# Stick-breaking attention weights as running products, two heads' logits from 64 rows each, and finishes issued in later parts

## The chip, the cores and the metric

The kernel runs on one core of a Trainium2 chip. The metric is the device time of one execution in microseconds (us). Engines are named as the profile names them: PE is TensorE (matmuls; PEld its weight loads), DVE is VectorE, ACT is ScalarE, POOL is GpSimd, SP is SyncE, whose queue issues most DMA transfers. A matmul of float32 operands shows in the trace as two passes, one of the rounded format fp32r as one.

## What is computed

One transformer layer on 512 tokens of width 1024 (16 meta tokens stand ahead of them): a projection, two mixers side by side (HGRN2 with 4 heads, stick-breaking attention with 8 heads of 64), the output projection with residual and layer norm, and a mixture of 16 experts with a second layer norm. The change touches the stick-breaking mixer and the two norms behind it.

```python
def head_rms_norm(x, g):
    xf = x.astype(jnp.float32)
    y = xf * lax.rsqrt(jnp.mean(xf * xf, axis=-1, keepdims=True) + RMS_EPS)
    return y.reshape(*x.shape[:-2], -1) * g

def stick_breaking_mixer(q, k, v, norm_g):
    ...
    for blk in range(Lp // Q_BLOCK):
        ...
        z = jnp.einsum('bhqd,bhkd->bhqk', qh[:, :, start:end], kh[:, :, :end])
        mask = jnp.arange(end)[None, :] < (start + jnp.arange(Q_BLOCK))[:, None]
        log_keep = jnp.where(mask, jax.nn.log_sigmoid(-z), 0.0)
        log_a = jax.nn.log_sigmoid(z) + lax.cumsum(log_keep, axis=3, reverse=True) - log_keep
        a = jnp.where(mask, jnp.exp(log_a), 0.0)
        outs.append(jnp.einsum('bhqk,bhkd->bhqd', a, vh[:, :, :end]))
    o = jnp.concatenate(outs, axis=2).transpose(0, 2, 1, 3)
    return head_rms_norm(o, norm_g)
```

So the weight of a key is sigmoid(z) of that key, times the product of sigmoid(-z) over all later keys that the query may see.

## The kernel before, in words

The kernel runs in stages: the input projection (7 groups of 512 columns), into whose last groups the HGRN2 heads are woven; then **the stick-breaking stage**, into which the output projection is woven (`weave`, ratio WO_RATIO); then the rest of the output projection with the router (which expert each token goes to); then the 16 experts, whose weights stream from HBM, and the second norm.

The stick-breaking stage has three units of query tiles (UNITS): tile 3 with 528 keys, tile 2 with 400, and tiles 0 and 1 together (144 and 272 keys, 416 columns). Within a unit the 8 heads go in pairs `pr` of two heads `s`; `sb_weights` makes one head's weights, `sb_values` transposes them (PE into bank `tr`, then a copy to the tile `aT`) and multiplies them with the values, and `sb_finish` normalises a group of heads and splits it in a high and a low half for the output projection. In the tiles, `z` of the code is a PSUM bank of the four named `pj`; `t` is the tag of `ll` (2 buffers), `zs` that of `cc` (3 buffers), `am` holds the weights of the meta keys.

The logits of one head are matmuls whose weights (`sqZ`) have 128 rows, of which 64 hold the head's query and 64 are zero, since the two heads of a pair share the 128 rows of `skT`. Each head then takes, on ACT, Abs, Exp, Ln and a last Exp, on DVE a Relu (a quarter of them on ACT), the reversed running sum (`tensor_tensor_scan`) and a subtraction from the logits, so that a `pj` bank is held until that subtraction. `rsqrt` is Ln and Exp on ACT with one Newton step on DVE in the norm of a token, and Ln and Exp alone in `sb_finish`.

`out_proj` multiplies the mixers' outputs with the output weights: `wo_half(0)` loads and splits the rows of the HGRN2 half, `wo_half(4)` those of the stick-breaking half; every product is three fp32r matmuls (`mm3`, lines L128 to L130, into banks `z`, for the last two token tiles also `pj`). `out_second` adds a token tile's products, transposes the tile and makes the router's logits and the norm's mean and deviation; `out_rows` applies the norm and writes the tile; `choose` and `rank` pick experts for two tiles at a time.

The order on every engine is set ahead of time by a scheduler which takes instructions by their place in the program, as buffers come free; each engine then works strictly in that order. `pump` queues the loads of expert weights on SP.

## Time and profile before

| | us |
|---|---|
| runs (3) | 697.75, 704.66, 706.35; median 704.66 |
| profiled execution, own time | 695.96 |
| its span, first to last instruction | 694.2 |
| PE busy | 652.1 (94%) |
| DVE busy | 524.6 (76%) |
| ACT busy | 412.4 (59%) |

Busy PE time counts matmuls whose modelled ends overlap, so that PE shows as busy even where it is not at its peak; the distance from one matmul's start to the next one's is the better price. The stick-breaking stage runs from about 234 us to 350 us, the router to about 369 us, the experts to about 660 us, the second norm to the end.

### The profile page before, as it was taken

Reading aid. Unit: us, or ns where it says so; the run is one execution under the profiler, and the core shown is the slowest. Engines: PE = TensorE matmul, PEld = TensorE weight load, DVE = VectorE, ACT = ScalarE, POOL = GpSimd, SP = SyncE. Lnnn points to the kernel's source line nnn. Section 1 sums busy time; section 2 is a strip of 40 time slices with the busy share of each in tenths; the row PEclk is TensorE's granted clock in tenths of the full one; section 3 lists DMA queues with packets and bytes.
Section 4 is the critical chain, followed back from the end, with each engine's and each line's share of the span. In section 5 each row is a group of like instructions: output and inputs, shape, how many; then the busy total and the mean of one; then the engine's idle time right before and its main releaser. Section 6 shows DMA issues by size and latency. Waiting matters only on the chain. (4 is left out here: it accounts for less than half of the span.)

```text
span 694.2 us, 9353 instructions
## 1 busy us (share of the span) xinstructions
PE 652.1 (94%) x3354; PEld 513.8 (74%) x3354; DVE 524.6 (76%) x836; ACT 412.4 (59%) x624; POOL 158.8 (23%) x177
## 2 busy tenths in 40 slices
PE   7999989999999999989978899999999999999983
PEld 6778867777778777778766678878778787787732
DVE  5353065675563796999779899999999999999484
ACT  5363333635262673855434778678688687698480
POOL 5210153343243100100001112333111141211301
PEclk9999999999999999999998999999999999999998
DMA  9532111011004880203567699999999999999641
GB/s 319 194 104 67 55 61 61 1 61 61 1 1 166 302 319 1 90 34 121 190 236 283 261 338 326 356 354 351 351 334 353 337 362 348 334 358 376 187 164 59
DMA packets 62451, 143.67 MB, mean 207 GB/s; under 512 B 7386, under 2 KB 7418, under 8 KB 62400
## 3 DMA queue, kind: packets, MB, share of 16 engines
q1 hardware_dynamic: 53312, 127.67, 50.9%
q0 software_dynamic: 5904, 12.82, 6.3%
q10 hardware_dynamic: 3184, 2.53, 1.2%
q8 instruction: 28, 0.46, 0.3%
q14 instruction: 23, 0.19, 0.1%
HBM read 137.01 MB, written 14.68 MB: 219 GB/s over the span
## 5 line engine op out<-in xcount | busy, mean ns | idle before, releaser
L923 DVE TENSOR_TENSOR b<-b 128x1024 fp32r<-128x1024 f32 x180 | 211.3, 1216 | 5.2 <-ACT b L922 5.1
L922 ACT ACTIVATE b<-b 128x1024 fp32r<-128x1024 f32 x180 | 177.6, 1054 | 7.8 <-PE pj L130 4.8
L128 PE MATMUL pj<-b 128*128 128x512 f32 x256 | 103.8, 407 | 2.3 <-ACT b L207 2.3
L129 PE MATMUL pj<-b 128*128 128x512 f32 x256 | 101.8, 397 | 0.5 <-DVE b L124 0.5
L130 PE MATMUL pj<-b 128*128 128x512 f32 x256 | 101.6, 398 | 0.0
L128 PE MATMUL pj<-b,xh 128*128 128x512 f32 x224 | 90.4, 404 | 0.2 <-ACT b L922 0.2
L129 PE MATMUL pj<-b,xl 128*128 128x512 f32 x224 | 88.2, 394 | 0.6 <-DVE xl L1243 0.6
L130 PE MATMUL pj<-b,xh 128*128 128x512 f32 x224 | 87.4, 408 | 0.8 <-DVE b L923 0.8
L124 DVE TENSOR_TENSOR b<-b 128x1024 fp32r<-128x1024 f32 x24 | 32.4, 1357 | 47.7 <-ACT b L339 44.0
L984 POOL DMA_INDIRECT xg<-h1d,idx x15 | 20.9, 1393 | 174.7 <-DVE gate L981 71.0
L128 PEld LDWEIGHTS pj<-b 128*128 128x128 f32 x256 | 48.3, 189 | 14.2 <-ACT b L207 2.6
L130 PEld LDWEIGHTS pj<-b 128*128 128x128 f32 x256 | 48.5, 190 | 10.6 <-issue 0.7
L129 PEld LDWEIGHTS pj<-b 128*128 128x128 f32 x256 | 48.6, 190 | 10.3 <-DVE b L124 0.9
L130 PEld LDWEIGHTS pj<-b,xh 128*128 128x128 f32 x224 | 42.6, 190 | 11.8 <-DVE b L923 3.1
L339 ACT ACTIVATE b<-b 128x1024 fp32r<-128x1024 f32 x28 | 29.3, 1059 | 35.6 <-PE pj L130 21.6
L1033 POOL DMA_INDIRECT ad<-y,idx x14 | 41.0, 2926 | 38.9 <-ACT b L922 30.4
L129 PEld LDWEIGHTS pj<-b,xl 128*128 128x128 f32 x224 | 42.5, 190 | 9.8 <-DVE xl L1243 1.0
L128 PEld LDWEIGHTS pj<-b,xh 128*128 128x128 f32 x224 | 42.8, 191 | 8.7 <-ACT b L922 1.5
L640 ACT ACTIVATE zs<-zs 128x512 f32<-128x512 f32 x28 | 17.7, 631 | 45.9 <-POOL zs L639 45.8
L122 POOL TENSOR_TENSOR b<-b 128x1024 fp32r<-128x1024 f32 x8 | 21.1, 2636 | 84.6 <-ACT b L339 65.6
L638 POOL TENSOR_TENSOR zs<-u 128x256 f32<-128x256 f32 x28 | 21.2, 756 | 59.5 <-issue 19.1
L641 DVE TENSOR_TENSOR zs<-zs,u 128x256 f32<-128x256 f32 x28 | 14.3, 510 | 21.7 <-ACT zs L640 21.6
(359 smaller groups left out, 1279.1 us busy)
## 6 DMA issues: line engine op xcount, KB each, us to landing
b<-in_w_exp_gate_dram SPq DMA_DIRECT2D x32, 1024.0 KB, 8.2
b<-in_w_exp_up_dram SPq DMA_DIRECT2D x32, 1024.0 KB, 10.2
b<-in_w_exp_down_dram SPq DMA_DIRECT2D x32, 1024.0 KB, 9.8
b<-in_w_in_dram SPq DMA_DIRECT2D x12, 1024.0 KB, 4.9
b<-in_w_out_dram SPq DMA_DIRECT2D x4, 1024.0 KB, 4.8
b<-in_x_dram SPq DMA_DIRECT2D x7, 512.0 KB, 7.6
b<-in_w_in_dram SPq DMA_DIRECT2D x4, 512.0 KB
h1d<-b POOLq DMA_DIRECT2D x4, 512.0 KB, 3.7
```

The source lines that it names most:

```text
L122: nc.gpsimd.tensor_sub(dst, src, hi)
L124: V.tensor_sub(dst, src, hi)
L128: nc.tensor.matmul(acc, ah, bh, start=first, stop=False)
L129: nc.tensor.matmul(acc, al, bh, start=False, stop=False)
L130: return nc.tensor.matmul(acc, ah, bl, start=False, stop=last)
L339: latest[0] = nc.scalar.activation(wt[:, 0], src, AF.Copy).ins
L638: nc.gpsimd.tensor_sub(xv[:, :, 0, :], ref, bv[:, :, 0, :])
L640: nc.scalar.activation(X, X, AF.Exp)
L922: latest[:] = (nc.scalar.activation(t[:, 0], raw, AF.Copy).ins, V.tensor_sub(t[:, 1], raw, f32(t[:, 0])).ins)
L923: V.tensor_sub(t[:, 1], raw, f32(t[:, 0])).ins)
L984: nc.gpsimd.indirect_dma_start(out=dst, out_offset=None, in_=h1d, in_offset=bass.IndirectOffsetOnAxis(ap=idx, axis=0), bounds_check=T - 1, ...
L1033: nc.gpsimd.indirect_dma_start(out=ad, out_offset=bass.IndirectOffsetOnAxis(ap=idx, axis=0), in_=y, in_offset=None, bounds_check=T - 1, oo ...
```

## The change

The weights are no longer made through logarithms. ACT makes sigmoid(-z) and sigmoid(z) straight from the logits, DVE makes the reversed running product of the first (a scan with a multiplication, and a minimum that changes nothing), and one product of the two, shifted by one key, gives the weights. The subtraction that held the `pj` bank is gone, and so are Abs, Relu, Exp, Ln and Exp; the copy of the transposed weights to `aT` goes from DVE to ACT. A sigmoid table is loaded once ahead of the stage, and the log-exp table isn't there any more, so that both norms take their reciprocal square root on DVE: a first guess by integer arithmetic on the bits, and three Newton steps (`rsqrt`).

The queries are stored once (`sqT`, no zeros), and the two heads of a pair use rows 0 to 63 and 64 to 127 of the PE, one matmul behind the other (`sb_logits`).

`sb_finish` and `out_second` become generators: the second part of each is issued later, behind other work of the program. 

```diff
     def ev_sq(c, acc):
-        if c % 2 == 0:
+        if c == 0:
             t = big_tile(4)
-            sqZ.extend(t[:, j] for j in range(4))
-        for s in range(2):
-            q_ = sqZ[2 * c + s]
-            r, o = slice(64 * s, 64 * s + 64), slice(64 * (1 - s), 64 * (1 - s) + 64)
-            nc.gpsimd.memset(q_[o], 0.0)
-            if s:
-                nc.scalar.activation(q_[r], acc[r], AF.Copy, scale=0.125)
-            else:
-                V.tensor_scalar(q_[r], acc[r], 0.125, None, op0=OP.mult)
+            sqT.extend(t[:, j] for j in range(4))
+        nc.scalar.activation(sqT[c], acc, AF.Copy, scale=0.125)
...
+    def rsqrt(y, v, u, scale, eps):
+
+        V.tensor_scalar(v, v, scale, eps, op0=OP.mult, op1=OP.add)
+        V.tensor_scalar(y.bitcast(I32), v.bitcast(I32), -0.5, 1597463007.0, op0=OP.mult, op1=OP.add)
+        V.tensor_scalar(v, v, -0.5, None, op0=OP.mult)
+        for _ in range(3):
+            if v.shape[1] == 1:
+                V.tensor_scalar(u, y, y, v, op0=OP.mult, op1=OP.mult)
+            else:
+                V.tensor_mul(u, y, y)
+                V.tensor_mul(u, u, v)
+            V.scalar_tensor_tensor(y, u, 1.5, y, op0=OP.add, op1=OP.mult)
...
+    def sb_logits(pr, qts, spans, n):
+
+        pieces = [], []
+        rows = [slice(64 * s, 64 * s + 64) for s in range(2)]
         if n == 528:
             for a in range(2):
-                z = pj()
-                nc.tensor.matmul(z[:, 0:264], sqZ[h][:, 384:512], skT[pr][:, 264 * a:264 * a + 264],
-                                 start=True, stop=not a)
-                pieces.append((z, 264 * a, 264))
-            nc.tensor.matmul(z[:, 136:264], identb, maskb, start=False, stop=True)
+                z = [pj(), pj()]
+                for s, r in enumerate(rows):
+                    nc.tensor.matmul(z[s][:, 0:264], sqT[pr][r, 384:512], skT[pr][r, 264 * a:264 * a + 264],
+                                     start=True, stop=not a)
+                    pieces[s].append((z[s], 264 * a, 264))
+            for s in range(2):
+                nc.tensor.matmul(z[s][:, 136:264], identb, maskb, start=False, stop=True)
...
         ll, cc = tt(), tt("zs", ZS_BUFS)
-        relu[0] += RELU_SHARE
-        for z, a, w in pieces:
-            nc.scalar.activation(ll[:, a:a + w], z[:, 0:w], AF.Abs)
-            if relu[0] // 8 != (relu[0] - RELU_SHARE) // 8:
-                nc.scalar.activation(cc[:, a:a + w], z[:, 0:w], AF.Relu)
-            else:
-                V.tensor_scalar(cc[:, a:a + w], z[:, 0:w], 0.0, None, op0=OP.max)
-        nc.scalar.activation(ll[:, 0:n], ll[:, 0:n], AF.Exp, scale=-1.0)
-        nc.scalar.activation(ll[:, 0:n], ll[:, 0:n], AF.Ln, bias=1.0)
+        with tc.issue_after(sigmoid_table[0]):
+            for z, a, w in pieces:
+                nc.scalar.activation(ll[:, a:a + w], z[:, 0:w], AF.Sigmoid, scale=-1.0)
+                nc.scalar.activation(cc[:, a:a + w], z[:, 0:w], AF.Sigmoid)
         for a, b in spans:
             rv = slice(b - 1, a - 1 if a else None, -1)
-            V.tensor_tensor_scan(cc[:, rv], cc[:, rv], ll[:, rv], 0.0, op0=OP.add, op1=OP.add)
-        for z, a, w in pieces:
-            V.tensor_sub(cc[:, a:a + w], z[:, 0:w], cc[:, a:a + w])
-        nc.scalar.activation(cc[:, 0:n], cc[:, 0:n], AF.Exp)
+            V.tensor_tensor_scan(ll[:, rv], ll[:, rv], ll[:, rv], 1.0, op0=OP.mult, op1=OP.min)
+
+        V.tensor_mul(cc[:, 0:n - 1], cc[:, 0:n - 1], ll[:, 1:n])
...
             aT = quad(tt("aT", AT_BUFS, 512))
-            V.tensor_copy(aT[:, 0:w], p_[:, 0:w])
+            nc.scalar.activation(aT[:, 0:w], p_[:, 0:w], AF.Copy)
...
             sb_values(prs.index(pr), pr, prs, st["o"], zz, qts, spans)
+            for f in ends[:]:
+                ends.remove(f)
+                next(f, None)
             if pr == prs[-1]:
-                sb_finish(am, st["o"], prs, qts)
+                ends.append(sb_finish(am, st["o"], prs, qts))
+                next(ends[-1])
...
+        behind, st_ = iter(()), {}
         for i in (3, 2):
             acc = [zb(), zb()]
             for n_ in range(4):
                 wo_mm(i, 4, wo, acc, (n_,))
+                next(behind, None)
+                if i == 2 and n_ == 3:
+                    out_rows(3, st_[3])
                 yield 1
-            out_rows(i, out_second(i, acc, 1))
+            behind = out_second(i, acc, 1, st_)
+            next(behind)
             yield 1
+        for _ in behind:
+            yield 1
+        out_rows(2, st_[2])
         choose(2)
         rank(2)
...
     pump(R_FREE)
+    sigmoid_table.append(tables("sigmoid_and_others"))
     weave(stick_breaking(), out_proj(), WO_RATIO)
...
-    st_ = [out_second(i, acc2[i], 0) for i in (0, 1)]
+    st_ = {}
+    both_ = [out_second(i, acc2[i], 0, st_) for i in (0, 1)]
+    for _ in range(3):
+        for f in both_:
+            next(f, None)
```

The scheduler's order moves with it, in three places. On SP the two loads of the output weights' first half (`in_w_out`) stand directly behind the input projection's loads before:

```order
L183 DMA b<-in_w_in_dram 128x4x512 x12
L730 DMA b<-in_w_out_dram 128x2x1024 x2
L894 DMA b<-in_w_exp_gate_dram 128x4x512
L894 DMA b<-in_w_exp_up_dram 128x4x512
L894 DMA b<-in_w_exp_gate_dram 128x4x512
```

After, on the same queue, from the fourth of the seven early pieces of expert weights on:

```order
L919 DMA b<-in_w_exp_up_dram 128x4x512
L919 DMA b<-in_w_exp_gate_dram 128x4x512
L919 DMA b<-in_w_exp_up_dram 128x4x512
L919 DMA b<-in_w_exp_gate_dram 128x4x512
L745 DMA b<-in_w_out_dram 128x2x1024 x2
L859 DMA b<-in_x_dram 128x1024 x4
L745 DMA b<-in_w_out_dram 128x2x1024 x2
```

The output weights' loads moved behind all seven pieces of expert weights. On PE, at the start of the stage, the first matmuls of the output projection (`z<-b`) stand among the first logits (`pj<-skT,b`) before:

```order
L128 MATMUL z<-b 128x512
L129 MATMUL z<-b 128x512
L504 MATMUL pj<-skT,b 128x264
L130 MATMUL z<-b 128x512
L504 MATMUL pj<-skT,b 128x264
L507 LDWEIGHTS identb
L507 MATMUL pj<-maskb,identb 128x128
L128 MATMUL z<-b 128x512
L504 MATMUL pj<-skT,b 128x264
L129 MATMUL z<-b 128x512
L504 MATMUL pj<-skT,b 128x264
```

After, the stage begins on PE with logits alone (the masks' matmuls are those with `identb`):

```order
L509 MATMUL pj<-skT,b 128x264 x3
L513 LDWEIGHTS identb
L513 MATMUL pj<-maskb,identb 128x128
L509 MATMUL pj<-skT,b 128x264
L513 LDWEIGHTS identb
L513 MATMUL pj<-maskb,identb 128x128
L509 MATMUL pj<-skT,b 128x264 x3
```

and the first matmul of the output projection comes behind nearly the whole unit of 528 keys and the logits of two pairs of the next unit:

```order
L551 MATMUL tr<-ident,zs 128x128 x4
L521 LDWEIGHTS identb
L521 MATMUL pj<-maskb,identb 128x128
L521 LDWEIGHTS identb
L521 MATMUL pj<-maskb,identb 128x128
L127 MATMUL z<-b 128x512
L128 MATMUL z<-b 128x512
```

So the output projection no longer fills the first unit on PE. On DVE, at the end of the stage, the sums of the last two token tiles (`b<-b,z` and `b<-b,pj`) are followed at once by their statistics before:

```order
L478 TENSOR_TENSOR b<-pj,b 128x256
L757 TENSOR_TENSOR b<-b,z 128x512 x2
L259 BN_STATS st<-b 128x6 x2
L757 TENSOR_TENSOR b<-b,pj 128x512
L261 BN_AGGR mv<-st 128x2
L757 TENSOR_TENSOR b<-b,pj 128x512
L251 TENSOR_SCALAR mv<-mv 128x1
L771 SCALAR_TENSOR_TENSOR lg<-nws,mv,z 128x20
```

After, the norm of token tile 2 (the two operations of 128x1024), its logits and the choice of experts for tiles 2 and 3 (`gt<-lg`) stand between them:

```order
L481 TENSOR_TENSOR b<-pj,b 128x256
L773 TENSOR_TENSOR b<-b,z 128x512 x2
L773 TENSOR_TENSOR b<-b,pj 128x512
L271 BN_STATS st<-b 128x6
L795 SCALAR_TENSOR_TENSOR b<-b,mv 128x1024
L789 SCALAR_TENSOR_TENSOR lg<-nws,mv,z 128x20
L796 SCALAR_TENSOR_TENSOR b<-b,mv 128x1024
L790 SCALAR_TENSOR_TENSOR lg<-lg,mv,lgb 128x20
L773 TENSOR_TENSOR b<-b,pj 128x512
L812 TENSOR_TENSOR gt<-lg 128x160
```

What `out_rows(2)` and `choose(2)` do moved from the middle of the stage to its end.

## Rows read from the trace of the kernel before

**Rows 1.** Windows: length; busy PE, PEld, DVE, ACT, POOL (count); clock; DMA; GB/s.
```profile
233.50:262.00 28.50, 26.61 (x150) 20.96 (x150) 25.36 (x46) 21.48 (x47) 2.16 (x8) 1.00 0.84 330
262.00:350.00 88.00, 82.88 (x493) 66.33 (x493) 73.24 (x154) 48.22 (x101) 8.88 (x17) 1.00 0.28 99
358.60:362.00 3.40, 0.69 (x12) 0.42 (x10) 3.37 (x17) 2.11 (x3) 0.00 (x0) 1.00 0.00 0
362.00:365.40 3.40, 1.69 (x10) 1.41 (x11) 3.40 (x7) 0.00 (x0) 0.00 (x0) 0.81 0.00 0
390.00:640.00 250.00, 246.15 (x1199) 196.79 (x1199) 241.92 (x313) 194.67 (x230) 58.66 (x27) 0.99 0.98 347
```

**Rows 2.** Timeline of PE, first unit: start, duration, instruction.
```profile
251.95 1.16 PE L504 MATMUL pj<-skT,b 128*128 128x264 f32 x4 [0.27 <-DVE zs L529]
252.94 0.22 PE L507 MATMUL pj<-maskb,identb 128*128 128x128 bf16 x1
...
261.38 0.39 PE L129 MATMUL z<-b 128*128 128x512 f32 x1
261.60 0.39 PE L130 MATMUL z<-b 128*128 128x512 f32 x1
```

**Rows 3.** Timeline of DVE, first unit: one head, and the unit's last row.
```profile
253.09 1.25 DVE L527 TENSOR_TENSOR_SCAN zs<-zs,t 128x528 f32<-128x528 f32 x1
254.26 0.40 DVE L522 TENSOR_SCALAR zs<-pj 128x264 f32<-128x264 f32 x1
254.59 0.76 DVE L529 TENSOR_TENSOR zs<-pj,zs 128x264 f32<-128x264 f32 x2
...
255.61 0.67 DVE L545 COPY aT<-tr 128x512 f32<-128x512 f32 x1
256.20 1.24 DVE L527 TENSOR_TENSOR_SCAN zs<-zs,t 128x528 f32<-128x528 f32 x1
...
261.10 0.77 DVE L529 TENSOR_TENSOR zs<-pj,zs 128x264 f32<-128x264 f32 x2
```

**Rows 4.** Timeline of PE, projection: eight passes on four tiles of 32 columns.
```profile
24.84 0.39 PE L130 MATMUL pj<-b 128*128 128x512 f32 x1
25.15 1.07 PE L372 MATMUL z<-b,xm 128*32 128x512 f32 x8
26.15 0.50 PE L128 MATMUL pj<-b 128*128 128x512 f32 x1
```

**Rows 5.** Timeline of the SP queue: issues of DMAs.
```profile
218.54 3.90 SPq L730 DMA_DIRECT2D b<-in_w_out_dram  x2
...
241.88 0.37 SPq L894 DMA_DIRECT2D b<-in_w_exp_gate_dram  x1
```

**Rows 6.** Timeline of DVE, router: waits, small operations in a chain and side by side.
```profile
353.75 0.23 DVE L771 SCALAR_TENSOR_TENSOR lg<-nws,mv,z 128x20 f32<-128x20 f32 x1 [1.56 <-PE z L768]
...
357.55 0.23 DVE L771 SCALAR_TENSOR_TENSOR lg<-nws,mv,z 128x20 f32<-128x20 f32 x1 [1.86 <-PE z L768]
...
357.96 0.27 DVE L252 TENSOR_SCALAR mv<-mv 128x1 f32<-128x1 f32 x1
358.27 0.16 DVE L253 SCALAR_TENSOR_TENSOR mv<-mv 128x1 f32<-128x1 f32 x1
...
358.73 0.32 DVE L795 TENSOR_TENSOR gt<-lg 128x160 f32<-128x160 f32 x1
...
360.10 0.16 DVE L801 TENSOR_SCALAR ohg<-cnt 128x8 f32<-128x8 f32 x1
360.17 0.17 DVE L804 TENSOR_SCALAR top<-cnt 128x32 f32<-128x32 f32 x1
```

**Rows 7.** Timeline of ACT, first expert: a table load between two operations.
```profile
384.58 1.05 ACT L922 ACTIVATE b<-b 128x1024 fp32r<-128x1024 f32 x1
385.65 1.28 ACT L1084 ACT_TABLE_LOAD   x1
386.95 0.60 ACT L1084 ACTIVATE hs<-pj 128x512 f32<-128x512 f32 x1
```

More of the change, by code (lines that the diff above doesn't have):

```diff
@@ L56 @@
 EARLY = 2
-RELU_SHARE = 2
 ZS_BUFS = 3
@@ L130, in mm3, with tables @@
         return nc.tensor.matmul(acc, ah, bl, start=False, stop=last)
-    def log_exp_tables():
-        i_ = nc.scalar.preload_act_table_set(NLE)
+    def tables(name=NLE):
+        i_ = nc.scalar.preload_act_table_set(name)
         i_ = getattr(i_, "ins", i_)
         before = [o for o in nc.cur_bb.bb.instructions if o is not i_ and o.engine == i_.engine]
-        for o in before[-32:]:
+        for o in before[-64:]:
             tc.add_manual_dep(i_, o.name, mybir.DependencyInfo(mybir.DependencyClass.NoSync,
@@ L508, in sb_weights @@
         else:
-            z = pj()
+            z = [pj(), pj()]
             for i, (a, b) in zip(qts, spans):
-                nc.tensor.matmul(z[:, a:b], sqZ[h][:, i * P:(i + 1) * P], skT[pr][:, 0:b - a],
-                                 start=True, stop=False)
-                nc.tensor.matmul(z[:, b - P:b], identb, maskb, start=False, stop=True)
-            pieces.append((z, 0, n))
-        ll, cc = tt(), tt("zs", ZS_BUFS)
-        relu[0] += RELU_SHARE
-        for z, a, w in pieces:
-            nc.scalar.activation(ll[:, a:a + w], z[:, 0:w], AF.Abs)
-            if relu[0] // 8 != (relu[0] - RELU_SHARE) // 8:
-                nc.scalar.activation(cc[:, a:a + w], z[:, 0:w], AF.Relu)
-            else:
-                V.tensor_scalar(cc[:, a:a + w], z[:, 0:w], 0.0, None, op0=OP.max)
@@ L523, in sb_weights @@
-        nc.scalar.activation(ll[:, 0:n], ll[:, 0:n], AF.Exp, scale=-1.0)
-        nc.scalar.activation(ll[:, 0:n], ll[:, 0:n], AF.Ln, bias=1.0)
+                for s, r in enumerate(rows):
+                    nc.tensor.matmul(z[s][:, a:b], sqT[pr][r, i * P:(i + 1) * P], skT[pr][r, 0:b - a],
+                                     start=True, stop=False)
+                for s in range(2):
+                    nc.tensor.matmul(z[s][:, b - P:b], identb, maskb, start=False, stop=True)
+            for s in range(2):
+                pieces[s].append((z[s], 0, n))
@@ L567, in sb_finish @@
         nc.scalar.activation(t, o[:, 0:n], AF.Square)
-        rs = att.tile([P, 8], F32, tag="rs", bufs=2, name="rs")[:, 0:n // 64]
-        V.tensor_reduce(rs, heads(t), axis=AX.X, op=OP.add)
-        nc.scalar.activation(rs, rs, AF.Ln, scale=1.0 / 64.0, bias=eps_rms)
-        nc.scalar.activation(rs, rs, AF.Exp, scale=-0.5)
+        sums, rs, u = (att.tile([P, 8], F32, tag=tag, bufs=2, name=tag)[:, 0:n // 64] for tag in ("ss", "rs", "ru"))
+        V.tensor_reduce(sums, heads(t), axis=AX.X, op=OP.add)
+        rsqrt(rs, sums, u, 1.0 / 64.0, RMS_EPS)
         V.tensor_mul(heads(t), heads(o), rs[:, :, None].to_broadcast([P, n // 64, 64]))
+        yield 1
         p_ = pj([P, 4, P])
@@ L582, in stick_breaking @@
     def stick_breaking():
-        todo = []
+        todo, ends = [], []
         st = {}
@@ L600, in stick_breaking @@
                     zz = []
+                    pieces = sb_logits(pr, qts, spans, n)
                     for s in range(2):
-                        zz.append(sb_weights(pr, s, am, qts, spans, n))
+                        zz.append(sb_weights(pr, s, pieces[s], am, qts, spans, n))
                         yield 1
@@ L612, in stick_breaking @@
         drain()
+        for f in ends:
+            next(f, None)
     def chunks(ap):
@@ L716, in hymba_kernel @@
                 feature_constants() if n == 9 else router_constants()
-    with tc.issue_after(log_exp_tables()):
+    with tc.issue_after(tables()):
         for h in range(HH):
@@ L751, in hymba_kernel, with out_second @@
     gb1, acc2, h1 = [], {}, {}
-    def out_second(i, acc, first):
+    def out_second(i, acc, first, stats_):
         r = rt_[i]
@@ L1356, in hymba_kernel @@
             then(i_.ins)
-            then(log_exp_tables())
+            then(tables())
             for i in range(NT):
```

21 lines of the change are left out of this document (11 added, 10 removed).

## The prediction

> **What bounds the kernel now.** I read the page first: PE is busy 94% of the span, DVE 76%, ACT 59%, so a gain has to come out of PE's work or its waits. The windows by stage come next [rows 1]. The experts hold PE for 246.15 of 250.00 us with the DMA engines at 0.98: nothing of the change is in that stretch, so it starts earlier or later by what the stages ahead of it give, and runs as long as now. From 262 us to 350 us PE is busy 82.88 of 88.00 us; that part has 5.1 us of idle time at most. Third, the timelines of the first unit (528 keys), which is another case: there DVE sets the pace. One head takes DVE from 253.09 to 256.20, 3.11 us (running sum 1.25, two Relus of 0.40, two subtractions 0.76, half a copy of `aT` each 0.67), and the logits of the next head wait for its subtraction, 0.27 us before the row at 251.95 [rows 2, 3]. The last DVE row of the unit ends at 261.87 [rows 3]. PE isn't lost meanwhile: between the logits it runs passes of the output projection, which start 0.22 us apart (261.38, 261.60) [rows 2]. Counted in the timeline, 37 of them lie ahead of 262 us, 37 x 0.23 = 8.5 us.
>
> So the unit that gets much faster is one whose spare PE time is already filled, and the unit's end is not what counts. What counts is when PE is through with all that must precede the router.
>
> **The first unit.** Abs, Relu, Exp, Ln, Exp and the subtraction go; a sum becomes a product of the same shape, 1.25 us, and the weights' product reads two tiles of 528 columns: by the two subtractions of 264 columns, 0.76 us together, at most that, and I take 0.65 for one instruction in place of two [rows 3]. A head then costs DVE 1.9 us where it was 3.11, and eight heads 15.2 us. ACT has four sigmoids of 264 columns and half the unit's copy of `aT`; at DVE's 0.40 to 0.42 us for 264 columns and 0.67 for a copy of 512, with starts closer than durations, some 1.7 us a head: beside DVE, not ahead of it. PE has 26.61 us of busy time in 28.50 us now, of which 8.5 us are the output projection [rows 1]; the other 18 us are 4.5 us a pair. The logits of a head are four passes in 0.99 us (251.95 to 252.94) [rows 2], a pair's eight in 2.0; two heads side by side need 1.0 us and two changes of tiling. The only tiles in the trace are 32 columns wide: eight passes of 512 columns take 1.00 us (25.15 to 26.15), where eight in turn would take 8 x 0.23 = 1.8 at the least. So tiles do run beside each other, and the matmul ahead of them took 0.31 instead of 0.23 [rows 4]; with the exit I charge 0.2 us a visit. PE then needs about 3.7 us a pair, 15 us for the unit: level with DVE.
>
> The Trainium skill, page "TensorEngine Tiling (Array Packing)", section Key Properties, says that tiles work independently, but also that a change of the tiling mode drains TensorE. The rows above agree with both and price the drain at 0.2 us; rows of 64 are in no trace here.
>
> The first running product needs logits, a table and two sigmoids. Logits begin at about 234 us, as the stage does; a table load takes 1.28 us, with 0.02 us of idle time on either side of it [rows 7]. The Trainium skill, "ScalarE: Activation LUTs", section What ACT_TABLE_LOAD costs, adds a drain of 1.38 us to a load of 1.28; these rows show no such drain, and by the page the start would be 1.4 us later. I take 236.5 us for the first scan, so that DVE leaves the unit at 236.5 + 15.2 = 252, ten microseconds ahead of 261.87.
>
> **What PE is owed then.** Today the loads of the output weights issue at 218.54, and the expert pieces up to 241.88 [rows 5]. Now the weights stand behind all those pieces, so they land at about 248 us and are split on ACT and DVE behind the unit's work: no product of the output projection before about 256. All 37 passes are pushed behind the unit. From 252, PE has: the 88 us that follow 262 now, plus 8.5 us, minus what the logits of the other two units save. Those are eight heads of 400 and eight of 416 columns in two passes each; at 0.99 / 4 / 264 = 0.94 ns a column [rows 2] that is 8 x 816 x 2 x 0.94 ns = 12.3 us, of which half, 6.1, goes, less 12 visits to tiles at 0.2 us, 2.4: 3.7 us. The sum is 252 + 88 + 8.5 - 3.7 = 344.8 us for the end of the stage, where it is 350. Idle PE time of 5.1 us goes in part too, since the values no longer wait for a copy on a busy DVE (ACT, 48.22 of 88 [rows 1], takes it): I give that 1.3 us. The output projection's absence between 252 and 256 costs nothing as long as the next unit's logits are there; the order has two pairs of them. **End of the stage 343.5, 6.5 us earlier.**
>
> **DVE and the small operations.** Reciprocal roots move from ACT to DVE: five finishes of 12 operations and two norms of 9 in the stage, 78. Small operations side by side start 0.07 us apart (360.10, 360.17); in a chain 0.31 (357.96 to 358.27), or two steps in 0.46 (358.27 to 358.73, one row between), so 0.23 to 0.31 [rows 6]. In the order about 50 of them stand in bare chains and the rest between other work, so 50 x 0.26 + 28 x 0.1 = 16 us; the ends are 78 x 0.07 = 5 and 78 x 0.31 = 24. Against it go 16 copies (about 0.5 us each, 8) and the Relus of units 1 and 2 (6 us); splitting half of the output weights later brings some 4 us in. 73.24 - 8 - 6 + 4 + 16 = 79 us [rows 1], in a stretch of 91.5 us: not the bound, and its cover is PE's output projection. Each finish of 12 x 0.26 = 3 us does stand ahead of the next scan; PE has products to run then, and if it had none, five finishes would cost up to 15 us.
>
> **The tail.** From the stage's end at 350 to the choice at 358.73 [rows 6] it is 8.7 us. Now token tile 2's norm (two operations of 128x1024, 1.2 us each), its logits and its choice stand on DVE between the last sums, and each of two last norms has four more small operations in a row. That is 2.4 + 2 + 1 = 5.4 us more on DVE, of which the 1.56 and 1.86 us that DVE waits now for the router's logits [rows 6] take a good part. I take +2, between 0 and +5. The two other table loads (1.28 each [rows 7]) fall into that time on ACT and ahead of the stage.
>
> The clock: granted 1.00 (2.4 GHz) in all of the stage, 0.81 in one stretch of 3.4 us, right after one in which PE was busy 0.69 us of 3.40 [rows 1]. The half level costs only where PE idles as long as that; the start of the stage is the one place, and I put nothing on it.
>
> **Sum.** 695.96 - 6.5 + 2 = 691.5 us for the profiled execution. The median of the runs shown is 704.66, 8.7 us above that execution, so the forecast is 704.66 - 4.5 = 700, to the nearest half.
>
> **Rivals.**
> A, PE's waits vanish as well: logits no longer hold a bank until DVE is through with it. With all 5.1 us of idle time gone, changes of tiling free (2.4) and a tail hidden entirely, the stage ends at 344.8 - 5.1 - 2.4 = 337.3 and the time falls by 12.7, up to 14 with an earlier start: 691. For it: the wait on `pj` in [rows 2]. Against: most of the 88 us have products to fill any wait.
> B, the change doesn't do what it says: the two halves run one after the other. Then no logit time goes, and 16 visits cost 3.2 us; the first unit is 4.7 us a pair on PE (ends at 254), the other two keep their 12.3. End: 254 + 88 + 8.5 + 2.4 - 1.3 = 351.6, tail +2: about 4 us slower, 708. For it: no row of such tiles. Against: [rows 4].
> C, slower: the chains of small operations. If each costs 0.31 us wherever it stands, with waits between scan and finish that no product covers, because PE works strictly in order and the values behind it need that scan, the five finishes cost PE 5 x 12 x 0.31 = 18.6 us less 6.5 gained, and the tail +4: 704.66 + 12 + 4 = 720 at worst; half of that exposed, 711. It decides from the point at which more than 8 us of the finishes are uncovered. For it: contiguous chains in the order, DVE at 79 of 91.5. Against: finishes are issued ahead of other pairs' work, and 192 passes of output projection, 44 us, are to be had for cover.
>
> **How the numbers follow.** Two per cent, 14 us, is about what a measurement of this kernel can tell from no change. Forecast 0.52 (694 to 705), A 0.22, B 0.13, C 0.13. A's 691 lies at the bound of 14 us, so half of it passes, 0.11, and 0.03 of the forecast's lower tail with it: faster 0.14. C is past +14 only where nearly all is exposed, half of it: with a little of B, slower 0.08. Same 0.78. The range goes from 687, a little below A, to 711, where C is half exposed; it leaves out a third of A, most of what C has above 711 and B's upper end, a fifth in all.
>
> **What would show it.** First scan at 236.5 and 1.9 us between heads; DVE out of the first unit at 252; the first `z` product at about 256; logits of two heads starting together and four rows taking half their 0.99 us; the last product of the output projection at 343.5; the choice 10.7 us behind it; the first expert's matmul 4 to 5 us earlier. Right mechanism, wrong size would be a later unit end or a longer tail. Wrong altogether: logits one behind the other (B), PE waiting on a scan that stands behind a chain of root operations (C), or a PE at half clock in the first unit, which I have not priced.

## The result, and the profile after

The changed kernel takes 738.21 us (median of 4 runs, 735.57 to 743.39), the kernel before 702.65 in the same session: a ratio of 1.052, 95% interval 1.0427 to 1.0612. It is slower by 36 us, where I had forecast 700. The profiled execution of the changed kernel took 743.39 us, the slowest of its four, with a span of 741.7; the one of before, 695.96, lies below all timed runs of that kernel, so spans compare badly and I compare places in the program. The choice of experts for tiles 0 and 1 starts at 394.76 (before 358.73, [rows 6]), and the experts' first product at 405.9 (before 369.3). So 36.7 of the 47.5 us between the two spans are there when the experts begin; the other 10.8 come behind (335.8 us from that product to the end, where it was 324.9).

The windows of the changed kernel, with the columns of [rows 1]; the third is a stretch inside the first two:

```profile
233.50:262.00 28.50, 27.88 (x102) 18.35 (x100) 16.14 (x18) 14.96 (x40) 7.59 (x8) 0.56 0.94 370
262.00:350.00 88.00, 78.44 (x380) 58.47 (x378) 53.01 (x130) 31.43 (x59) 7.72 (x12) 0.85 0.16 52
237.40:272.00 34.60, 33.22 (x119) 23.50 (x119) 18.95 (x21) 15.20 (x37) 8.23 (x11) 0.50 0.66 261
```

PE is busier than before in the first unit (27.88 against 26.61 of 28.50 us) and does less: its granted clock is 0.50, the lower level of 1.2 GHz, from 237.4 to about 272 us. Busy share alone hides that. DVE, which set the pace of this unit, falls from 25.36 to 16.14 us. The PE timeline of the changed kernel shows where the clock fell, and where the output projection came:

```profile
232.76 1.15 PE L509 MATMUL pj<-skT,b 64*128 64x264 f32 x6
...
235.50 1.94 PE L509 MATMUL pj<-skT,b 64*128 64x264 f32 x6 [0.62 <-ACT zs L533]
...
239.84 2.13 PE L509 MATMUL pj<-skT,b 64*128 64x264 f32 x6
...
269.65 0.80 PE L127 MATMUL z<-b 128*128 128x512 f32 x1 [1.39 <-ACT b L754]
...
296.73 0.94 PE L518 MATMUL pj<-skT,b 64*128 64x400 f32 x4
297.60 0.28 PE L521 MATMUL pj<-maskb,identb 128*128 128x128 bf16 x2
```

Six passes take about 1.1 us at 232.76 and 2.1 at 239.84. Between them PE was idle once, for 0.62 us. The two heads do run side by side: at the full clock four passes of 400 columns take 0.87 us (296.73 to 297.60), where the same four from 128 rows take 1.35 (249.88 to 251.23 in e17_full_rows_late, shown below). On DVE and ACT the start of the unit is as forecast:

```profile
235.76 1.26 DVE L536 TENSOR_TENSOR_SCAN t<-t 128x528 f32<-128x528 f32 x1 [8.21 <-ACT t L532]
237.12 0.71 DVE L538 TENSOR_TENSOR zs<-zs,t 128x527 f32<-128x527 f32 x1
237.75 1.25 DVE L536 TENSOR_TENSOR_SCAN t<-t 128x528 f32<-128x528 f32 x1
...
256.94 1.26 DVE L536 TENSOR_TENSOR_SCAN t<-t 128x528 f32<-128x528 f32 x1 [6.77 <-ACT t L532]
...
258.95 1.25 DVE L536 TENSOR_TENSOR_SCAN t<-t 128x528 f32<-128x528 f32 x1
260.33 0.71 DVE L538 TENSOR_TENSOR zs<-zs,t 128x527 f32<-128x527 f32 x1
```

```profile
233.48 1.28 ACT L132 ACT_TABLE_LOAD   x1
234.77 0.39 ACT L532 ACTIVATE t<-pj 128x264 f32<-128x264 f32 x1
```

The first scan is at 235.76, a head takes 1.99 us (3.11 before, [rows 3]), and the table load is followed by the first sigmoid with 0.01 us between. Then the slow PE starves DVE: 6.77 us of waiting ahead of the seventh head, so that DVE is through with the unit at 261.04 (260.33 and 0.71). The SP queue (issues) has the output weights behind the last expert piece, where [rows 5] had them at 218.54:

```profile
242.24 0.37 SPq L919 DMA_DIRECT2D b<-in_w_exp_gate_dram  x1
242.66 1.01 SPq L745 DMA_DIRECT2D b<-in_w_out_dram  x2
```

In the third unit there is a second fall of the clock. Here DVE has a finish (`L577`, the sum of squares, to `L579`, the product with the root), PE a wait for a scan and one for that product, and the windows the clock:

```profile
321.39 0.69 DVE L577 TENSOR_REDUCE ss<-t 128x8 f32<-128x512 f32 x1 [1.91 <-ACT t L575]
...
322.36 0.15 DVE L256 TENSOR_SCALAR ss<-ss 128x8 f32<-128x8 f32 x1
322.42 0.72 DVE L536 TENSOR_TENSOR_SCAN t<-t 128x272 f32<-128x272 f32 x1
323.05 0.15 DVE L257 TENSOR_SCALAR rs<-ss 128x8 int32<-128x8 int32 x1
...
328.30 0.15 DVE L265 SCALAR_TENSOR_TENSOR rs<-ru,rs 128x8 f32<-128x8 f32 x1
...
328.52 0.69 DVE L579 TENSOR_TENSOR t<-oT,rs 128x512 f32<-128x512 f32 x1
```

```profile
325.84 0.90 PE L551 MATMUL tr<-ident,zs 128*128 128x128 f32 x3 [1.35 <-DVE t L536]
329.27 2.82 PE L558 MATMUL oT<-b,aT 128*128 128x64 f32 x12 [2.53 <-DVE t L579]
```

```profile
323.00:332.00 9.00, 4.48 (x22) 3.61 (x21) 8.09 (x35) 2.29 (x5) 0.00 (x0) 0.66 0.01 2
332.00:339.50 7.50, 7.50 (x31) 5.31 (x30) 3.92 (x9) 2.83 (x6) 0.00 (x0) 0.50 0.00 0
```

Small operations alone are short; the same timeline has the last finish's sum, its first small operation, its twelfth and its product:

```profile
372.62 0.42 DVE L577 TENSOR_REDUCE ss<-t 128x4 f32<-128x256 f32 x1 [1.22 <-ACT t L575]
373.08 0.17 DVE L256 TENSOR_SCALAR ss<-ss 128x4 f32<-128x4 f32 x1
...
375.13 0.16 DVE L265 SCALAR_TENSOR_TENSOR rs<-ru,rs 128x4 f32<-128x4 f32 x1
375.39 0.42 DVE L579 TENSOR_TENSOR t<-oT,rs 128x256 f32<-128x256 f32 x1
```

From sum to product that is 2.8 us (2.3 from the first small operation on). The finish at 321.39 takes 7.1 us (6.2), since scans, products and statistics stand between its twelve small operations on DVE. PE is busy half the time (4.48 of 9.00 us), and after that runs at half its clock for another 7.5 us. A third fall comes behind a wait for the sum of a token tile (`L773`), which DVE reaches at 349.29, behind one more finish (343.31 to 348.38) and two scans:

```profile
350.00 1.11 PE L781 MATMUL z<-ident,b 128*128 128x128 f32 x4 [2.21 <-DVE b L773]
```

```profile
350.00:363.00 13.00, 12.74 (x54) 11.76 (x55) 6.71 (x15) 2.28 (x4) 1.32 (x2) 0.50 0.24 97
```

The last product of the output projection starts at 383.1 us (349.8 before); the forecast had it done at 343.5.

### The profile page after: what moved, and what is told of

Read it like the earlier page. It is cut to its first block, busy times and chain, and to the rows that moved or that the text cites. A ratio compares the mean times of both kernels' runs of the same rounds, so it can differ in the third digit from the quotient of the medians.

```text
span 741.7 us, 9338 instructions
## 1 busy us (share of the span) xinstructions
PE 685.6 (92%) x3354; PEld 533.0 (72%) x3354; DVE 512.2 (69%) x860; ACT 393.1 (53%) x584; POOL 168.8 (23%) x169
## 5 line engine op out<-in xcount | busy, mean ns | idle before, releaser
L948 DVE TENSOR_TENSOR b<-b 128x1024 fp32r<-128x1024 f32 x180 | 211.1, 1217 | 3.7 <-ACT b L947 3.7
L123 DVE TENSOR_TENSOR b<-b 128x1024 fp32r<-128x1024 f32 x24 | 35.3, 1481 | 42.3 <-ACT b L349 41.9
L1014 POOL DMA_INDIRECT xg<-h1d,idx x15 | 24.6, 1639 | 153.9 <-DVE gate L1011 80.4
L1063 POOL DMA_INDIRECT ad<-y,idx x14 | 46.0, 3286 | 57.2 <-ACT b L947 28.0
L129 PEld LDWEIGHTS pj<-b 128*128 128x128 f32 x256 | 48.2, 188 | 10.8 <-issue 0.7
L536 DVE TENSOR_TENSOR_SCAN t<-t 128x528 f32<-128x528 f32 (+3 forms) x32 | 27.5, 874 | 19.6 <-ACT t L532 19.6
```

The lines of the kernel that those rows point to most:

```text
L123: V.tensor_sub(dst, src, hi)
L129: return nc.tensor.matmul(acc, ah, bl, start=False, stop=last)
L536: V.tensor_tensor_scan(ll[:, rv], ll[:, rv], ll[:, rv], 1.0, op0=OP.mult, op1=OP.min)
L948: V.tensor_sub(t[:, 1], raw, f32(t[:, 0])).ins)
L1014: nc.gpsimd.indirect_dma_start(out=dst, out_offset=None, in_=h1d, in_offset=bass.IndirectOffsetOnAxis(ap=idx, axis=0), bounds_check=T - 1, ...
L1063: nc.gpsimd.indirect_dma_start(out=ad, out_offset=bass.IndirectOffsetOnAxis(ap=idx, axis=0), in_=y, in_offset=None, bounds_check=T - 1, oo ...
```

## The experiments

All ratios are against runs of the kernel before on the same chip. Two kernels differ clearly where their intervals don't overlap. "Late" output weights are issued behind all seven expert pieces. "Early" is at the head of the queue with 128 rows everywhere (issued at 217 to 220 us), but behind two pieces (227 to 230 us) with rows of 64 or in e19.

| kernel | rows of a head's logits | output weights | finishes, token rows | us | ratio, 95% interval |
|---|---|---|---|---|---|
| changed | 64 | late | deferred | 738.21 | 1.052 (1.0427 to 1.0612) |
| e17_full_rows_late | 128 | late | deferred | 726.2 | 1.0343 (1.0273 to 1.0412) |
| e2_weights_early | 64 | early | deferred | 729.51 | 1.0382 (1.031 to 1.0454) |
| e1_full_rows | 128 | early | deferred | 719.75 | 1.0281 (1.0203 to 1.0359) |
| e5_filled | 64, filled | late | deferred | 731.93 | 1.0418 (1.0348 to 1.0488) |
| e6_short_roots | 64 | late | deferred | 729.89 | 1.0384 (1.0333 to 1.0434) |
| e3_not_deferred | 64 | late | whole | 718.06 | 1.0205 (1.0165 to 1.0246) |
| e11_rows_early_whole | 64 | early | whole | 716.35 | 1.017 (1.0105 to 1.0236) |
| e7_weights_alone | 128 | early | whole | 707.28 | 1.0062 (1.0038 to 1.0086) |
| e18_rows_early_short | 64 | early | whole | 705.58 | 1.0069 (1.0036 to 1.0101) |
| e19_first_unit_full | 128, then 64 | early | whole | 708.63 | 1.0112 (1.0075 to 1.0148) |
| e8_short_roots_whole | 128 | early | whole | 700.07 | 0.9943 (0.991 to 0.9977) |
| with logarithms: | | | | | |
| e4_rows_alone | 64 | late | whole | 713.22 | 1.0166 (1.0109 to 1.0224) |
| e10_weights_late | 128 | late | whole | 709.61 | 1.01 (1.0065 to 1.0134) |
| e13_rows_and_early | 64 | early | whole | 715.22 | 1.0157 (1.0092 to 1.0221) |
| e16_rows_after_first | 128, then 64 | late | whole | 718.96 | 1.0263 (1.022 to 1.0306) |
| e9_deferral_alone | 128 | early | deferred | 715.28 | 1.0165 (1.0126 to 1.0203) |
| e14_finishes_deferred | 128 | early | finishes deferred | 704.17 | 1.0037 (1.0003 to 1.0071) |
| e15_rows_deferred | 128 | early | rows deferred | 708.76 | 1.0096 (1.0076 to 1.0116) |

Three theories stood against each other at first. **Rows**: logits from 64 rows pull the clock down. **Cover**: the output projection, gone from the first unit, leaves PE too little to do. **Order** and **chains**, for what comes behind: deferred work that others wait for, or the twelve small operations of a root.

### Rows or cover

**e1_full_rows** stores the queries with zeros again, and its weights' loads fall back to the front of the queue by themselves.

```diff
-nc.tensor.matmul(z[s][:, 0:264], sqT[pr][r, 384:512], skT[pr][r, 264 * a:264 * a + 264],
+nc.tensor.matmul(z[s][:, 0:264], sqT[2 * pr + s][:, 384:512], skT[pr][:, 264 * a:264 * a + 264],
```

> The changed kernel with the logits of each head from all 128 rows again (64 of them zero, stored as before), which also brings the output weights' loads back to the front of the SP queue. If the rows of 64 pull the clock down (theory of rows), the granted clock stays at 1.00 from 236 us to 270 us and the time comes back to between 700 and 712 us. If the missing output projection does it (theory of cover), the clock stays at 1.00 too, since its products stand among the first logits again; then the kernel with early output weights and rows of 64 must be as good. If neither, the clock falls to 0.50 in the first unit here as well and the time is 735 to 745 us.

The clock stays at 1.00 (237.4 to 272 us), and 2.4 points of the 5.2% go, where the theory of rows had 700 to 712 us. The remaining 2.8% have another cause.

**e2_weights_early** loads the first half of the output weights ahead of the call that queues expert pieces.

```diff
+    for g in range(2):
+        raw0.append(big_tile(2))
+        nc.sync.dma_start(raw0[g], rap(w_out, 2 * g * P * D, [[D, P], [P * D, 2], [1, D]]))
     slots.extend([free] * R_FREE + [big] * (R_LATE + R_AFTER))
     pump(R_FREE)
```

> The changed kernel with rows of 64, but the first half of the output weights loaded behind two expert pieces and not behind seven, so that products of the output projection stand in the first unit. Theory of cover: the clock stays at 1.00 from 238 us to 270 us, the first unit ends at about 252 us and the time falls by 15 us or more, below 723 us. Theory of rows: the clock still falls to about 0.5 in stretches where logits of 64 rows and transposes run, and the time stays above 728 us.

8.7 us less, with intervals that overlap a little. The clock is 0.79 and 0.53 in the windows from 235 to 245 us, back at 1.00 some 4 us after the first products (from 240.16), and 0.66 once more from 265 to 270. Between both expectations.

**e5_filled** adds work that nobody reads.

```diff
+        z = zb()
+        for _ in range(4):
+            nc.tensor.matmul(z, fl[0][:, 0:P], fl[0], start=True, stop=True)
```

> The changed kernel with 32 matmuls of 512 columns more in the first unit, four behind each head's weights, whose result nobody reads: 32 x 0.23 = 7.4 us of PE work at the full clock. Theory of cover: the clock stays at 1.00 from 237 us to 270 us, and the kernel gets faster by doing more, 715 to 732 us. Theory of rows: the clock falls all the same and the added work costs 7 to 15 us, 745 to 755 us.

32 matmuls more, and 6 us less between the medians: each of its four runs lies below each of the changed kernel's, but the intervals of the ratios overlap. The windows of this kernel:

```profile
237.40:257.00 19.60, 19.31 (x118) 13.25 (x118) 14.47 (x15) 13.61 (x39) 6.78 (x7) 1.00 1.04 402
257.00:268.00 11.00, 8.98 (x40) 6.96 (x39) 5.90 (x8) 4.27 (x7) 1.47 (x4) 0.69 0.65 250
```

With matmuls of 128 rows and 512 columns between them the logits of 64 rows run at the full clock; where the filling ends, the clock falls. That speaks for cover, or for rows that need it.

**e4_rows_alone**, **e10_weights_late** and **e13_rows_and_early** try both on the kernel with logarithms: the first with `sb_logits` and `ev_sq` of the change, the second with the loads' order alone, the third as the first with the loads of e2.

```diff
+            if not base:
+                tc.add_manual_dep(d_.ins, loads[R_FREE - 1].name, ...
```

> The kernel before with one part of the change alone: queries without zeros and the logits of two heads from 64 rows each; weights through logarithms, finishes and norms as before. Its output weights come behind seven expert pieces too, so cover is missing in the first unit as in the changed kernel. Theory of rows: the clock falls to about 0.5 in the first unit, and the time is 715 to 735 us. Theory of cover: the same, since both are there; the kernels with early weights and with filled idle time tell these two apart. If the loss lies in the order of the new weights and finishes alone: clock at 1.00 and 695 to 705 us.

> The kernel before with one edit: the output weights' first half is loaded behind all seven expert pieces, as in the changed kernel, so that the first unit has logits from 128 rows but no output projection beside them. With the kernels of rows 64 alone (713.22 us, clock 0.50 in the first unit) and of before (702.5, clock 1.00) it fills a table of rows against cover. Theory of cover: the clock falls to 0.50 in the first unit here too, 709 to 716 us. Theory of rows: the clock stays at 1.00 or dips for a few microseconds only, 700 to 707 us.

> The kernel before with logits from rows of 64, and the output weights' first half loaded behind two expert pieces, so that products of the output projection stand in the first unit. The fourth field of the table. Theory of cover: clock at 1.00 in the first unit and 697 to 705 us, the halved logits being worth a few microseconds. Theory of rows: clock about 0.5 to 0.8 there in spite of the cover, 708 us or more.

e10 has the clock at 0.61 and 0.71 in the ten microseconds from 235 on, behind a wait of 3.03 us, and at 1.00 from 245, though its first product of the output projection starts at 258.6. e4 stays at 0.50 from 240 until 260. So far rows; but e13 is no better than e4, and its PE timeline tells why:

```profile
242.64 2.53 PE L499 MATMUL pj<-skT,b 64*128 64x264 f32 x8 [5.06 <-DVE zs L532]
```

The logits of two heads take all four `pj` banks at once, and with logarithms a bank is held until DVE's subtraction. The pair waits 5.06 us: a cost of pairing with the old weights, which the changed kernel hasn't got. (The single head of e10 waits 3.03 us at its place.) **e16_rows_after_first** has pairs too and waits 3.28 and 2.22 us in the first unit for such subtractions, so that its time (719 us, above both forecasts' bounds of 707 and 709) decides nothing. What it shows is the clock: 1.00 in all windows from 265 to 345 us, with rows of 64 beside products.

> The kernel before with rows of 64 in the second and third unit only, where products of the output projection stand beside them; the first unit has 128 rows. Its output weights load behind all expert pieces, so it is to be read against the kernel with these late weights and 128 rows everywhere (709.61 us) and the one with 64 rows everywhere (713.22 us). If rows of 64 cost nothing but the clock of a bare first unit, the halved logits of 16 heads give 3 to 4 us back: 705 to 707 us, the clock in the first unit as with 128 rows. If they pull the clock down beside products too, 709 us or more, with stretches below 1.00 between 265 us and 345 us.

**e17_full_rows_late** is the clean test: e1 with the loads held behind the seven pieces, by the dependency above. Against the changed kernel only the rows differ (and with them how the queries are stored).

> The changed kernel with logits from 128 rows and the output weights' first half held behind all seven expert pieces, as in the changed kernel: with products for weights the fourth field of the table of rows (64 or 128) against cover (late or early). The others took 738.21 (64, late), 729.51 (64, early) and 719.75 us (128, early). Theory of cover: the clock falls to 0.50 from 238 us to 270 us as in the changed kernel, and the time is 733 us or more. Theory of rows: the clock dips for a few microseconds at the start of the unit at most and comes back without any product of the output projection, and the time is 720 to 728 us.

Its window, the first logits on PE, four passes of 400 columns and the first product of the output projection:

```profile
237.40:259.60 22.20, 20.63 (x140) 16.31 (x138) 18.26 (x22) 16.01 (x41) 9.10 (x12) 1.00 0.90 353
```

```profile
236.33 1.85 PE L516 MATMUL pj<-skT,b 128*128 128x264 f32 x6 [1.22 <-ACT zs L540]
...
249.88 1.51 PE L525 MATMUL pj<-skT,b 128*128 128x400 f32 x4
251.23 0.28 PE L528 MATMUL pj<-maskb,identb 128*128 128x128 bf16 x2
...
259.58 0.80 PE L127 MATMUL z<-b 128*128 128x512 f32 x1
```

No product of the output projection runs before 259.58, PE idles twice as long at this place as in the changed kernel (1.22 against 0.62 us), and the clock is 1.00 throughout. The unit's last scan starts at 251.4, not at 258.95, and the first product 10.1 us earlier than in the changed kernel (269.65). It isn't one execution's luck: the mean granted clock was 0.934 to 0.942 in the four runs of the changed kernel and 0.958 to 0.963 in the four of e17. Theory of rows holds for the clock: 1.8 points, 12 us, with intervals that don't meet. Cover is worth 0.6 with 128 rows (e17 to e1) and 1.4 with 64 (changed to e2), both with intervals that overlap; with the old weights its absence alone costs 1.0 (0.65 to 1.34, e10).

**e18_rows_early_short** and **e19_first_unit_full** ask the same with early weights, whole finishes and one step of Newton's, the second with zero-padded queries for the first unit only.

> The changed kernel with whole finishes, early output weights and one step of Newton's in each root (the last two refinements are left out); logits from 64 rows everywhere. With three steps it took 716.35 us; the shorter chains took 7 to 8 us off twice: 708 to 710 us. It is the base of the next kernel.

> The kernel with whole finishes, early output weights and short roots, with logits from 128 rows in the first unit only and from 64 in the other two. Theory of rows: the clock stays near 1.00 in the first unit, 8 us or more faster than with 64 rows everywhere, near the 700 us of 128 rows everywhere, and 3 to 4 us below that if the halved logits of 16 heads are a gain beside products. If the rows don't matter in the first unit: within 3 us of the kernel with 64 rows everywhere.

e19 missed: the clock is at 1.00 there, and the time the same or 3 us more. In e18 the clock is low in the windows from 235 to 245 (0.70 and 0.62), though products run from 239.57 on; in e19 PE idles instead (3.47 and 3.32 of 5 us busy from 240 to 250, with two waits of 1.53 and 1.68 us for DVE's split of the output weights), and the last scans of the unit start at 259.1 and 260.6. So with these early weights 128 rows in the first unit alone gain nothing. Rows of 64 aren't free beside products all the same: e8, with 128 rows everywhere, is 1.3 points below e18 (6 us between the medians, and 9 below e19), with intervals far apart. At the start of the second unit both fall below the full clock once more (0.73 and 0.66 from 265 to 270), behind one pair's logits from 64 rows and a wait of 1.58 and 1.71 us; e8 keeps 1.00 through a wait of 1.58 us at that place (260.15). How much of the 1.3 points that is, and why 64 rows don't give the 3.7 us, stays open: the output weights also load 9 to 10 us earlier in e8.

### Order and chains

**e3_not_deferred**, **e9_deferral_alone**, **e14_finishes_deferred**, **e15_rows_deferred**: the generators run through at once in the changed kernel, or are put into the kernel before, both or one.

```diff
-                ends.append(sb_finish(am, st["o"], prs, qts))
-                next(ends[-1])
+                for _ in sb_finish(am, st["o"], prs, qts):
+                    pass
```

> The changed kernel with finishes and token rows issued whole where they were before (rows of 64, products and roots on DVE stay). Theory of order (putting finishes, norms and tile 2's choice behind other work makes PE and the router wait): the time falls by 8 to 15 us, to 723 to 730 us, and the choice of experts comes within 9 us of the last product of the output projection instead of 12. Theory of chains (the twelve small operations of a root are what is waited for): within 4 us of the changed kernel, 734 to 742 us, or slower, since a chain is then waited for at once.

> The kernel before with one part of the change alone: finishes and token rows issued in later parts; weights and roots through logarithms, logits from 128 rows. Theory of order: 6 to 12 us slower than before, 707 to 713 us. Theory of chains: within 4 us of before, 697 to 705 us. The clock stays at 1.00 in the first unit under both.

> The kernel before with the second half of each finish issued behind the next pair's values, and nothing else of the change. All deferrals together cost 12.7 us. If the late finishes are what is waited for (the last products of the output projection need them), 708 to 715 us, and the last of these products ends 5 us or more later than at 350; if the token rows are, 700 to 705 us.

> The kernel before with the sums, norms, router logits and rows of the token tiles issued in later parts (so that tile 2's norm and the choice for tiles 2 and 3 come behind the stage), finishes whole. If the token rows cause the 12.7 us, 708 to 715 us, the first choice at about 360 us and not at 339.5, and the last 9 us or more later than at 359; if the finishes do, 700 to 705 us.

Undoing it gives 3.2 points (more than I expected), having it alone costs 1.65. Late finishes alone cost 0.4, late token rows 1.0: the rows are the greater part, and the sum, 1.3, is as much as 1.65 within the noise. In e15 the first choice moves from 339.5 to 358.8 us, as expected; but the last product of the output projection too is late, at 355.5 and not 349.8. PE of that kernel waits twice where before it waited once:

```profile
305.43 0.52 PE L543 MATMUL tr<-ident,zs 128*128 128x128 f32 x3 [2.15 <-DVE aT L545]
...
312.20 0.53 PE L543 MATMUL tr<-ident,zs 128*128 128x128 f32 x3 [1.36 <-DVE mv L261]
```

`mv` belongs to a token's norm, and the first wait was there before as well (2.09 us, at 303.59). Around the second, DVE's order is the same in both kernels: statistics, a finish's sum, a copy to `aT`, `mv`. What is gone is PE's own work. In the kernel before, the transposes and the router's logits of a token tile (`L764`, `L768`) fill this place:

```profile
305.59 0.60 PE L764 MATMUL z<-ident,b 128*128 128x128 f32 x4
...
307.87 1.92 PE L768 MATMUL z<-wr,b 128*128 128x20 f32 x16
309.63 0.53 PE L543 MATMUL tr<-ident,zs 128*128 128x128 f32 x3
```

Issued later, they no longer cover the finish. The windows there show 0.73 and 0.93 of the clock in e15 (305 to 315 us) and 1.00 before.

Where deferral costs its time differs by kernel. At the experts' first product the changed kernel is 13.6 us behind e3 (405.94, 392.38) and e9 12.9 behind the kernel before (382.20, 369.27), but e1 only 0.8 behind e7 (376.57, 375.73), though their spans are 9.8 us apart. In e1 the loss comes later, and part of it is a wait of PE for token rows gathered from HBM (`xg`):

```profile
390.78 0.69 PE L1091 MATMUL z<-ident,xg 128*128 128x128 f32 x2 [4.36 <-DMA xg<-h1d,idx]
```

That wait is 3.0 to 5.1 us in the six kernels with new weights and deferral, and 2.0 us or less in all others.

**e7_weights_alone** is the new weights and roots with nothing else; **e6_short_roots** and **e8_short_roots_whole** cut Newton's steps, in the changed kernel and in e7; **e11_rows_early_whole** is e2 with whole finishes.

```diff
-        for _ in range(3):
+        for _ in range(1):
```

> The kernel before with the new weights and the roots on DVE alone: logits from 128 rows, finishes and rows not deferred. The kernel with 128 rows and deferred finishes took 719.75 us. Theory of order: 700 to 710 us, most of those 19 us gone. Theory of chains: 715 to 725 us. If the new weights help by what I forecast for the first unit, and nothing else of the loss is theirs: 695 to 700 us.

> The changed kernel with one step of Newton's in each root and not three: a finish has 6 small operations instead of 12, a norm 5 instead of 9; it leaves out the last two refinements, so its outputs are a little less exact. 5 x 6 + 4 x 4 = 46 operations fewer. Theory of chains: 46 x 0.2 us = 9 us and what PE loses of its clock behind the waits, 718 to 730 us. Theory of order: within 4 us of the changed kernel, 734 to 742 us.

> The new weights with logits from 128 rows and whole finishes (707.28 us), with one step of Newton's in each root and not three, so that the last two refinements are left out. Where finishes are deferred this took 8 us off. If the chains are what the new weights lose by, 697 to 702 us, at or below the kernel before; if not, 705 to 709 us.

> The changed kernel with two things undone at once: finishes and token rows issued whole, and the output weights loaded behind two expert pieces; rows of 64, products and roots on DVE stay. Undoing the first alone took 20 us off the 738, the second alone 9 us. If the two losses are separate, 738 - 20 - 9 = 709 us; if one stands in the other's place, 715 us or more; the kernel with 128 rows and the same whole finishes took 707.28.

Two steps fewer, 46 operations, give 1.4 points in the changed kernel and 1.2 in e7 (8.3 and 7.2 us), and 1.0 from e11 to e18. e11 is 7 us above the sum of separate losses, as if partly one stood in the other's place, but the noise of four kernels is in that difference, so this isn't shown. e8 is faster than the kernel before, by 0.2 to 0.9%: the best version found, with roots that are a little less exact.

In e7, with no rows of 64 and no deferral, the unit of 528 keys ends 4.4 us earlier than before (last scan 255.4 against 259.8), and the stage ends 5 us later (last product at 354.9 against 349.8): PE waits 2.60 and 2.92 us for the product of a finish (at 308.23 and 331.28), and the clock is low around both (0.60 from 305 to 310, 0.50 from 330 to 335). In e8 these two waits are 1.13 and 0.31 us; the last product starts at 346.2 and the experts' first at 365.9, 3.6 and 3.4 us ahead of the kernel before.

The chain of single edits from e8 to the changed kernel, in per cent of the kernel before: new weights with short roots -0.6; two more steps in the roots +1.2; deferral +2.2; output weights late +0.6 (within the noise); rows of 64 +1.8; together 5.2.

## Why the prediction was wrong

- **The step that failed most plainly**: of the clock I wrote that "the half level costs only where PE idles as long as that; the start of the stage is the one place, and I put nothing on it". PE idled 0.62 us, and the clock was 0.50 for 34.6 us. Not idling did it but 64 rows without other work: 128 rows kept it through 1.22 us of idling (e17). It costs 12 us. The same sum had made PE and DVE level in the first unit; at half the clock PE set the pace, and DVE was through with the unit at 261.0 and not at 252.
- **Cover**: the output weights issued at 242.66, as forecast ("behind all those pieces"), but the first product came at 269.65 and not at 256, because they are split on ACT in order, at 268.55, behind a sigmoid that had waited 5.05 us for PE's transposes (at the full clock, in e17, it came at 259.58). "The output projection's absence between 252 and 256 costs nothing" was wrong in length; 4 to 10 us (e17 to e1, changed to e2, with intervals that overlap; e10's 7 us are clear of the noise).
- **The finishes**: "its cover is PE's output projection" failed. The price of a step was near: in a bare chain twelve operations took 2.3 us (373.08 to 375.39), 0.19 each, where I took 0.26. But a finish between other work took 7.1 us where the bare one took 2.8, PE waited, and the clock fell again. Rival C had this mechanism, with a price of up to 18.6 us and a chance of 0.13; short roots gave 8 us back.
- **Deferral** was costed only in the tail, +2. The tail came out so: from the last product to the choice 11.7 us, where it was 8.9 (383.1 to 394.76, 349.8 to 358.73). What I missed is the rest of the 11 to 22 us that deferral costs (e9, e3). In the stage, the router's matmuls that covered PE's waits were moved away (e15): the last product comes 7.3 us later in e9 than before. And "runs as long as now", of the experts, failed: from their first product to the end it took 332.7 to 337.1 us with new weights and deferral, 326.6 to 332.2 with new weights and without.
- **Right**: the first scan (235.76, forecast 236.5), 1.99 us a head (1.9), the logits side by side, with 0.2 us for the change of tiling as charged (0.87 against half of 1.35), so that rival B is out (only the price of a column was high: 0.84 ns at 400 columns, not 0.94); and the table load without a drain behind it. That the faster first unit is worth 4 to 5 us at the experts' first product is near what e8 gives (3.4), without rows of 64, deferral and two of three Newton steps. That 700 us came out for e8 is not the forecast come true: that kernel isn't the one that was forecast.
- Not settled: why the experts' first 40 us after a deferral are slow too (in e1 two windows of 10 us at a clock of 0.67). The wait for gathered rows is some 4 us of it; that these rows are written later is likely but not shown. The missing gain of rows of 64 beside products is open as well.

## What to carry to other kernels

Before a matmul is made smaller, ask what keeps PE's clock up in that stretch: halving the logits' rows in a unit without other work cost 12 us, and with 32 useless matmuls added the clock stayed up there (the 6 us that this seemed to give are within the noise). Price work moved to a second engine by where it stands in that engine's order, not by its own length: a finish of 2.8 us became one of 7.1 us with PE waiting. Before work of PE is issued later, look for the wait that it covers now. An edit that changes how many buffers or banks a step takes moves other things with it (here the output weights' loads, and with the old weights the banks of a pair), so test it with that held fixed.

## What the runs showed of the hardware

I hadn't expected the granted clock to tell 64 rows from 128: with no product of the output projection in either kernel, it was 0.50 from 237.4 us on with 64 rows, PE 96% busy (33.22 of 34.60 us), and 1.00 with 128, PE 93% busy (20.63 of 22.20). The Trainium skill, page "TensorE: Matmul & The Clock Gate", Part 1, says that the clock follows how busy PE has recently been; busy time as the profile counts it doesn't tell these two kernels apart, and the measurement decides. With matmuls of 128 rows and 512 columns between them, rows of 64 ran at 1.00 (e5, e16). Where one pair's logits from such rows were followed by transposes, the values' matmuls and a wait of 1.58 or 1.71 us, the clock fell (e18, e19); with 128 rows it stayed at 1.00 through 1.58 us there (e8). Two heads in rows of 64 took 0.87 us for four passes of 400 columns, 0.64 of the 1.35 us from 128 rows.
